# Layer 0's first MLP product by seven products, in two passes, and modulation chunks moved to its second product

## The chip, the cores and the metric

The kernel runs on one core of a Trainium2 chip. The metric is the device time of one execution in microseconds (us), as the median of several runs. PE is the engine for matrix products (its weight loads are shown as PEld), DVE and ACT are the vector and scalar engines, POOL is GpSimd, and SP is the engine whose queue issues the DMAs.

## What is computed

Two layers of a token-mixing sub-layer and an MLP, for 1024 latent tokens and 256 context tokens of 1024 features, in fp32. What the change touches is the MLP and the modulation vectors:

```python
def modulation(cvec, w_mod, b_mod):
    m = jax.nn.silu(cvec) @ w_mod + b_mod
    return jnp.split(m[:, None, :], N_MOD, axis=-1)
...
def sqrelu_mlp(h, w1, w2):
    a = jax.nn.relu(h @ w1)
    return (a * a) @ w2
...
        h2 = modulate(rmsnorm(xl_new, g_pre_mlp[i]), ml[3], ml[4])
        xl_new = xl_new + ml[5] * rmsnorm(sqrelu_mlp(h2, w_mlp_in[i], w_mlp_out[i]), g_post_mlp[i])
```

In layer 0 the MLP runs over the 10 token tiles of 128 (2 of context, 8 latent), in layer 1 over the 8 latent ones. W1 is 1024 x 4096, W2 is 4096 x 1024. Each modulation vector has 6 x 1024 entries for each layer and stream.

## The kernel before

Every fp32 operand is split into a high part, rounded to the type in which PE multiplies at one column per cycle, and a low part; a product is three matmuls (high x high, high x low, low x high, the helper mm3). A `split` is a cast on ACT and a subtraction on DVE.

All operands live in two arenas in SBUF: RT (split operands) and FT (fp32 values). The tables r_outp, r_up, r_down and the F_ tables give the columns of each stage's zones; a zone that is full, or columns that another zone still uses, make an instruction wait.

**Order of the work.** The kernel does not issue instructions as it is written. A Recorder collects them, finds what depends on what (by columns of 32), gives every instruction a cost, and lists them with a list scheduler for each engine (`walk`, eight times forwards and backwards, the best is kept). So the order on each engine is fixed when the kernel is built, and a change in one stage may move instructions in others. DMAs are all on SP's queue, which issues them in its listed order.

**The first MLP product.** In layer 1 it is computed by seven products (Strassen's scheme in Winograd's form, numbered 1 to 7) on pairs of token tiles and pairs of hidden blocks: with four pairs side by side the moving operand is 512 columns wide. W1's operands are made on the way (w1_ops: four sums on DVE and seven splits for each pair of hidden blocks j), `refill` keeps five ready. In layer 0 it is the plain product: for each of 32 hidden blocks f, token chunks of 4, 2 and 4 tiles, 8 x 3 matmuls each. Its token operands are built by `build_hT`, tiles 0 to 4 during the output product and 5 to 9 during the first blocks. In both layers the activations and four sums of them (strassen_sums) are stored to DRAM (actd), and four sums of W2's blocks as well (w2_sums: load, four DVE operations, store to tsd).

**The second MLP product** is seven products in both layers, in four groups g of four j. For each operand set `refill_down` loads activations and weights, splits them and keeps four sets ready; in layer 0 each set serves 5 x 3 matmuls of 512 columns.

**Modulation.** A chunk of 512 modulation columns (mod_task) is 8 loads of w_mod and 8 DVE operations for each stream (csil times a row, accumulated), then a split, matmuls with `pick`, and small transposes. In layer 0's first product twelve tasks run in the background: chunks 10 and 11 of layer 0 and all twelve of layer 1, 0 to 3 for two streams, and 4 to 11 for one. Chunks 0 and 1 are the next layer's first shift, 2 and 3 its scale; 10 and 11 are the gate of the MLP.

Of the kernel before, what the change touches and what calls it, by code (L numbers as in the profile page):

```python
# [46 lines left out]

PATTERN = "qvsvssvvvvsvssvvvvk", "vsvssvvvvsvssvvvvk"
# [8 lines left out]
def r_attn(x, y):  # L57
    return {"V": y, "K": (x[0], x[0] + 7680), "Q": (x[0] + 7680, x[1]), "PT": (28160, 31232), "AW": (31232, 34304), "WE": (20480, 26624), "WX": x, "S": (31232, 34304)}


def r_outp(x, y):
    return {"Y": y, "W": (26624, 28672), "S": (28672, 34304)}


def r_up(x, y):
    return {"Y": y, "X": x, "W": (20480, 34304)}


R_UP_LAST = {"W": (28672, 34304), **{f"H{q}": (7168 * q, 7168 * q + 7168) for q in range(4)}}


def r_down(x, y):
    return {"Y": y, "XT": x, "W": (20480, 34304)}
# [5 lines left out]
F_OUTP = {"Z": (3072, 14848), "C": (14848, 15616), "H": (15616, 16320)}  # L79
F_UP = {"A": (3072, 12032), "W2": (12032, 14080), "M": (14080, 16320), "H": (12032, 16320)}  # L80
F_UP_LAST = {"A": (3072, 10240), "S": (3072, 16320), "T": (10240, 14272), "W2": (14272, 16320)}
F_DOWN = {"Y": (3072, 13312), "H": (13312, 16320), "CS": (3072, 4352)}
# [197 lines left out]
class Arena:  # L280
# [15 lines left out]
    def alloc(self, cols, zone, room=0, top=False):  # L296
        need = -(-max(cols, room) // self.G)
        lo, hi = (c // self.G for c in self.zones[zone])
        if top:
            s = next((s for s in range(hi - need, lo - 1, -1) if not any(self.used[s : s + need])), None)  # L300
            if s is not None:
                return self.take(s, need, cols)
        cur = min(self.cursor.get(zone, lo), hi)
        for a, b in ((cur, hi), (lo, hi)):
# [30 lines left out]
def hybrid_backbone(ctx: ExitStack, tc: tile.TileContext, x, cx, cvec, vecs, lnrow, wmod, win, wq, wkv, wo, w1, w2, cs_tab, cst, out):  # L335
# [150 lines left out]
    def mod_task(l, hc, streams, pool_only=False):  # L486
# [26 lines left out]
        hls = [[R.alloc(512, "PT" if pool_only else "W") for _ in range(2)] for _ in accs]  # L513
# [237 lines left out]
    for l in range(depth):  # L751
# [544 lines left out]
        R.phase(r_outp(*xy))  # L1296
# [11 lines left out]
        HT = NP * P  # L1308

# [31 lines left out]
        tl = blks[0] + blks[1]  # L1341
        lds, mids = [], [wo_first(tl[1], wo_loads(tl[1]))]
        held, stiles, hreg = {}, {}, []

        RH = RT[:, 0:20480].rearrange("p (t s k c) -> p t s k c", t=10, s=2, k=KD)
        RS = RT[:, 0:28672].rearrange("p (q m s k c) -> p q m s k c", q=4, m=7, s=2, k=4)

        def tile_dest(k, grp):
            i = (grp[0] + TB) % 10
            return [RH[:, i : i + len(grp), s, k, :] for s in range(2)]  # L1350

        def pair_tile(q):

            xs = []
            for t in pairs[q]:
                xt = held.pop(t)
                ss, r = st(), st()
                nc.scalar.activation(junk, xt, AF.Square, accum_out=ss)
                rsq(r, ss, D)
                nc.vector.tensor_scalar(xt, xt, r, None, ALU.mult)  # L1360
                xs.append(xt)
            yield
            S = F.alloc(2048, "Z", top=True)
            S4 = S.rearrange("p (b k c) -> p b k c", b=4, k=4)
            A, B = ab_mlp[0]
            for kk in range(4):
                b = bank("hT")
                for i in range(4):
                    k = kk + 4 * (i // 2)
                    nc.tensor.transpose(b[:, i * P : (i + 1) * P], xs[i % 2][:, k * P : (k + 1) * P], ident)  # L1370
                for i in range(2):
                    k = kk + 4 * i
                    nc.scalar.activation(S4[:, 2 * i : 2 * i + 2, kk, :], v3(b[:, i * 256 : (i + 1) * 256], P), AF.Identity, bias=B[:, k : k + 1], scale=A[:, k : k + 1])
                yield
            for xt in xs:
                F.free(xt)
            stiles[q] = S

        def pair_ops(q, zone):

            S = stiles.pop(q)
            b11, b12, b21, b22 = (S[:, i * 512 : (i + 1) * 512] for i in range(4))
            t1, t2, t4 = (F.alloc(512, zone) for _ in range(3))

            def put(m, src):
                hi, lo = (RS[:, q, m - 1, s].rearrange("p k c -> p (k c)") for s in range(2))
                split(hi, lo, src)

            put(1, b11)
            nc.vector.tensor_sub(t1, b12, b11)  # L1390
            put(5, t1)
            nc.vector.tensor_sub(t2, b22, t1)
            put(6, t2)
            put(3, b22)
            nc.vector.tensor_sub(b12, b22, b12)
            put(7, b12)
            put(2, b21)
            nc.vector.tensor_sub(t4, b21, t2)
            put(4, t4)
            for a in (S, t1, t2, t4):  # L1400
                F.free(a)

        if last:
            hreg.append(R.alloc(7168, "Y"))
        else:
            hreg.append(R.alloc(KD * BLK, "Y"))
            s2 = Stream([(w1[l, f], 1, nc.vector) for f in range(2 * NPR)])
            s2.fill(1)
        for i, t in enumerate(tl):
# [14 lines left out]
            keep = last or t < TB  # L1424
            post(y, xt, G[0 if t >= 2 else 1], xmid[l][t * P : (t + 1) * P, :], keep=keep)
            if keep:
                held[t] = y
            if t == 1:
                F.free(G.pop(1))
            if last and t % 2:  # L1430
                builds.add(pair_tile(t // 2 - 1))
                if t == 5:
                    builds.drain()
                    pair_ops(0, "Z")
            elif not last and t < TB and (t % 2 or t == TB - 1):
                grp = [u for u in (t - 1, t) if u in held]
                builds.add(build_hT(None, grp, ab_mlp, tile_dest, "H", lo=nc.vector.tensor_sub, held=held))
# [10 lines left out]
        R.phase(R_UP_LAST if last else r_up(*xy))  # L1448

        def strassen_sums(A):  # L1450

            a11, a12, a22, s1, s2_, s3, s4 = (A[:, i * HT : (i + 1) * HT] for i in range(7))
# [5 lines left out]
        def store_act(j, A):  # L1458
            strassen_sums(A)
            nc.sync.dma_start(out=actd[l][j], in_=A)  # L1460
# [353 lines left out]
```

## Time and profile before

| | us |
|---|---|
| median of 3 runs | 2860.91 |
| their range | 2859.55 to 2861.93 |
| the profiled execution | 2859.87 |
| its span, first to last instruction | 2858.1 |

Stages in the profiled execution: layer 0's output product and first MLP product overlap around 734 us, the second product begins at 1218 us, and layer 1 at about 1573 us; layer 1's first product runs from 2228 to 2520 us and its second one to 2846 us. All instructions are recorded on one source line (L268, the call in `issue`), so the views are read by operation, tile and stretch of time and not by line.

### The profile page before, as it was taken

To read this page: it belongs to the slowest core of one execution; us is meant where nothing else is said; L and a number is where in the kernel's file an instruction comes from. 1 tells how busy PE (TensorE), PEld (TensorE's weight loads), DVE (VectorE), ACT (ScalarE), POOL (GpSimd) and SP (SyncE) were. 2 spreads that over 40 slices of the span, in tenths; PEclk is the share of its full clock that TensorE was granted. 3 is DMA by queue.
4 is the path that set the end of the run, shared out by engine and by line. 5 is a ranking of instruction groups with operands and counts; after the bars stand their busy time and mean duration, and the time that the engine had idled before them with its cause. 6 is when DMAs were issued, how large, how long until landed. Compare 5 with 4: busy or idle time off the path is not lost.

```text
span 2858.1 us, 41182 instructions
## 1 busy us (share of the span) xinstructions
PE 2766.9 (97%) x14978; PEld 2370.8 (83%) x14978; DVE 2143.6 (75%) x3578; ACT 1509.5 (53%) x2907; POOL 349.9 (12%) x363
## 2 busy tenths in 40 slices
PE   7999999989999999999999999999999899999998
PEld 4999888878888888888888799898877788878886
DVE  8988888888766654346666898888888877756777
ACT  6334777776533233353334834677767655554443
POOL 1015364822100000000000201000012000000001
PEclk9999999999999999999999899999999899999999
DMA  7213111254486787575555612000043576686664
GB/s 253 71 33 97 40 50 45 59 169 138 144 285 255 267 314 291 175 260 175 177 175 164 216 56 76 24 16 9 27 160 111 180 269 257 258 335 194 196 192 158
DMA packets 175411, 455.30 MB, mean 159 GB/s; under 512 B 18200, under 2 KB 43368, under 8 KB 167016
## 3 DMA queue, kind: packets, MB, share of 16 engines
q1 hardware_dynamic: 175208, 452.68, 47.2%
q8 instruction: 117, 1.92, 0.3%
q14 instruction: 86, 0.70, 0.1%
HBM read 324.58 MB, written 128.03 MB: 158 GB/s over the span
## 4 chain that ended last, share of the span: by engine, by line
PE 87%; DVE 6%; ACT 3%; DMA 2%; issue 1%; POOL 1%; SPq 0%; DVEq 0%; ACTq 0%
PE PS L268 87%; DVE RT L268 3%; DVE FT L268 2%; ACT FT L268 2%; ACT RT L268 1%; DVE stat L268 1%; POOL stat L268 1%; ACT junk L268 1%; DMA RT<-actd 0%; DMA FT<-in_wo_dram 0%; DMA FT<-in_w_dram 0%; DMA FT<-in_wmod_dram 0%; DMA FT<-atd 0%; SPq L268 0%; DMA FT<-rdd 0%
## 5 line engine op out<-in xcount | busy, mean ns | idle before, releaser
L268 PE MATMUL PS<-RT 128*128 128x512 f32 (+4 forms) x12884 | 2627.6, 359 | 39.1 <-ACT RT L268 19.0
L268 PEld LDWEIGHTS PS<-RT 128*128 128x128 f32 (+1 forms) x12884 | 2154.6, 189 | 373.8 <-ACT RT L268 27.2
L268 DVE TENSOR_TENSOR RT<-FT,RT 128x512 fp32r<-128x512 f32 (+5 forms) x724 | 496.4, 701 | 244.7 <-ACT RT L268 122.5
L268 ACT CAST RT<-FT 128x512 fp32r<-128x512 f32 (+3 forms) x648 | 411.1, 648 | 389.1 <-PE PS L268 312.9
L268 POOL TENSOR_TENSOR stat<-stat,nhalf 128x1 f32<-128x1 f32 (+2 forms) x147 | 125.5, 860 | 1942.0 <-ACT stat L268 1941.5
L268 PE MATMUL PS<-consts,FT 128*128 128x128 f32 (+2 forms) x2008 | 319.1, 275 | 39.1 <-ACT FT L268 15.5
L268 PEld LDWEIGHTS PS<-consts,FT 128*128 128x128 f32 (+2 forms) x2008 | 237.8, 142 | 94.2 <-ACT FT L268 26.9
L268 DVE TENSOR_TENSOR FT<-FT 128x512 f32<-128x512 f32 (+4 forms) x394 | 272.3, 720 | 52.1 <-DMA FT<-in_w_dram 33.6
L268 DVE TENSOR_TENSOR RT<-PS,RT 128x512 fp32r<-128x512 f32 (+3 forms) x409 | 264.5, 660 | 61.8 <-ACT RT L268 52.4
L268 ACT CAST RT<-PS 128x512 fp32r<-128x512 f32 (+3 forms) x409 | 226.1, 567 | 147.7 <-PE PS L268 137.5
L268 DVE TENSOR_TENSOR RT<-RT 128x640 fp32r<-128x640 f32 (+1 forms) x224 | 169.1, 756 | 130.9 <-ACT RT L268 124.6
L268 ACT ACTIVATE FT<-PS,stat 128x1280 f32<-128x1280 f32 (+3 forms) x218 | 216.4, 1003 | 63.3 <-POOL stat L268 25.3
L268 DVE TENSOR_TENSOR FT<-FT,PS 128x512 f32<-128x512 f32 (+3 forms) x350 | 205.5, 618 | 57.0 <-PE PS L268 42.0
L268 ACT CAST RT<-RT 128x640 fp32r<-128x640 f32 (+2 forms) x228 | 155.2, 682 | 161.5 <-DMA RT<-actd 150.6
L268 DVE SCALAR_TENSOR_TENSOR FT<-FT,vec 128x384 f32<-128x384 f32 (+2 forms) x440 | 221.8, 564 | 0.2
L268 ACT COPY FT<-PS 64x256 f32<-64x256 f32 (+9 forms) x258 | 120.0, 473 | 190.9 <-PE PS L268 186.8
L268 DVE TENSOR_REDUCE stat<-PS 128x1 f32<-128x1024 f32 (+1 forms) x200 | 203.9, 1024 | 13.2 <-PE PS L268 12.5
L268 ACT ACTIVATE FT<-PS 128x512 f32<-128x512 f32 (+3 forms) x126 | 65.3, 524 | 199.0 <-PE PS L268 191.7
L268 ACT ACTIVATE FT<-FT 128x512 f32<-128x512 f32 (+2 forms) x162 | 118.7, 736 | 52.0 <-DVE FT L268 49.4
L268 POOL TENSOR_TENSOR FT<-FT,csil 128x512 f32<-128x512 f32 x96 | 104.1, 1085 | 152.1 <-DVE RT L268 79.0
L268 DVE SCALAR_TENSOR_TENSOR FT<-FT,csil 128x512 f32<-128x512 f32 x140 | 99.7, 747 | 28.1 <-DMA FT<-in_wmod_dram 27.4
L268 POOL TENSOR_TENSOR FT<-FT 128x512 f32<-128x512 f32 x84 | 114.2, 1380 | 0.2
(59 smaller groups left out, 718.3 us busy)
## 6 DMA issues: line engine op xcount, KB each, us to landing
FT<-in_wmod_dram SPq DMA_DIRECT2D x160, 256.0 KB, 3.5
actd<-FT SPq DMA_DIRECT2D x16, 2240.0 KB
RT<-actd SPq DMA_DIRECT2D x112, 320.0 KB, 4.7
FT<-in_w_dram SPq DMA_DIRECT2D x64, 512.0 KB, 7.5
FT<-in_w_dram SPq DMA_DIRECT2D x32, 1024.0 KB, 5.6
tsd<-FT SPq DMA_DIRECT2D x32, 1024.0 KB, 8.4
FT<-tsd SPq DMA_DIRECT2D x128, 256.0 KB, 3.5
actd<-FT SPq DMA_DIRECT2D x16, 1792.0 KB, 7.6
```

The source lines that it names most:

```text
L268: r = getattr(getattr(self.nc, eng), name)(*args, **kw)
```

## The change

Layer 0's first product is done by the seven products too. Its pairs are a tile of the second half with one of the first half, (5,0), (6,1), (7,2), (8,3), (9,4). Pairs 0 to 2 are a first pass of 384 columns and pairs 3 and 4 a second pass of 256 columns; W1's operands are made in each pass. The output product takes its tiles in the order 0, 1, 5, 6, 2, 7, 3, 4, 8, 9, and `tile_blocks` builds blocks and operand sets of a pair when both its tiles are there: sets 1, 5, 6 and 3 early, and 7, 2 and 4 when the output product's weights are gone. The second pass's sets are built during the first pass, from xmid, starting at j = 9. W2's sums are spread by the table W2_AT, twelve in the first pass and four in the second, through one buffer of 2048 columns. Layer 1's first product uses the same new builder, with four pairs in one pass.

Of the modulation tasks one (layer 0, chunk 10) stays in the first product. The second product of layer 0 has layer 0's chunk 11 and layer 1's 0 to 9, and both gates and the next layer's affine rows as tasks between them; layer 1's chunks 10 and 11 go to layer 1's second product.

```diff
+W2_AT = {(0, 0): (0, 1), (0, 1): (2,), (0, 2): (3,), (0, 3): (4, 5), (0, 4): (6,), (0, 5): (7,), (0, 6): (8, 9), (0, 7): (10,), (0, 8): (11,), (1, 3): (12,), (1, 6): (13,), (1, 9): (14,), (1, 12): (15,)}
...
+R_OUTP = {"Y": (10240, 19456), "Y2": (31232, 34304), "W": (19456, 20480), "S": (26624, 31232)}
+R_UP = {"SL": (0, 9216), "W": [(9216, 10240), (19456, 23040)], "NY": (23040, 31232), "NX": (10240, 19456)}
...
+        groups = [[0, 1, 2, 3]] if last else [[0, 1, 2], [3, 4]]
...
+        MS = (1, 5, 6, 3, 7, 2, 4)
+        early = {1: "Y", 5: "Y"} if last else {1: "Y", 5: "Y", 6: "Y", 3: "Y2"}
...
+        def put(q, m):
+
+            g, i = place[q]
+            bl = blocks[q]
+            b11, b12, b21, b22 = bl
+            if m in (5, 6, 4):
+                nc.vector.tensor_sub(b11, {5: b12, 6: b22, 4: b21}[m], b11)
+            hi, lo = (slots[g][m][:, i * D + n * 512 : i * D + (n + 1) * 512] for n in range(2))
+            split(hi, lo, {3: b22, 7: b12, 2: b21}.get(m, b11))
+            if m == 3:
+                nc.vector.tensor_sub(b12, b22, b12)
...
-            for hc in range(10, 12):
-                mods.add(mod_task(0, hc, (0, 1)))
-            for hc in range(0, 4):
-                mods.add(mod_task(l + 1, hc, (0, 1)))
-            for hc in range(4, 12):
-                mods.add(mod_task(l + 1, hc, (0,)))
...
-            chunks_ = [(slice(5, 9), 1, 4), (slice(4, 10, 5), None, 2), (slice(0, 4), 0, 4)]
...
+            for l_, hc in ((l, 10),):
+                mods.add(mod_task(l_, hc, (0, 1), "NY"))
+        n_, start_next, n_next = 0, 9, 4
+        for g, grp in enumerate(groups):
+            w = len(grp) * P
...
+                for mi, (m, c) in enumerate(((1, 0), (5, 1), (6, 0), (3, 1), (7, 0), (2, 2), (4, 0))):
+                    refill(5 if last else 4)
...
+                        for n, (a, v) in enumerate(((wh, bh), (wh, bl), (wl, bh))):
+                            nc.tensor.matmul(v3(bs[c], P), a[:, s], v, start=m in (1, 5, 2) and kk + n == 0, stop=kk + n == 5, skip_group_check=True)
...
+                store_act(j, grp, A)
+                for j_ in (j,) if last else W2_AT.get((g, j), ()):
+                    w2_sums(j_)
...
+        if last:
+            for hc in (10, 11):
+                mods.add(mod_task(l, hc, (0,), "W"))
+        else:
+            ab_next = []
+            mods.add(mod_task(l, 11, (0, 1), "W"))
+            mods.add(both_gates())
+            for hc in range(4):
+                mods.add(mod_task(l + 1, hc, (0, 1), "W"))
+            mods.add(next_affine())
+            for hc in range(4, 10):
+                mods.add(mod_task(l + 1, hc, (0,), "W"))
```

PE's list where layer 0's first product begins, before (RT are split operands, PS is PSUM, 128x256 the output; the last transposes of the token tiles stand first):

```order
L268 MATMUL PS<-consts,FT 128x128 x2
L268 MATMUL PS<-RT 128x512 x9
L268 MATMUL PS<-RT 128x256 x24
L268 MATMUL PS<-RT 128x512 x24
L268 MATMUL PS<-RT 128x256 x24
L268 MATMUL PS<-RT 128x512 x24
```

And of the change, from the last tile of the output product to the first modulation task (its matmuls read `pick`):

```order
L267 MATMUL PS<-consts,FT 128x128 x6
L267 MATMUL PS<-RT 128x512 x48
L267 MATMUL PS<-RT 128x384 x223
L267 MATMUL PS<-RT,pick 2x512
L267 MATMUL PS<-RT 128x384 x51
```

The plain product began among transposes of its own token tiles; the new one begins after the last of them, and no other matmul of the output product stands behind it. Where the passes meet, and the second product begins, the change has on PE:

```order
L267 MATMUL PS<-RT 128x384 x114
L267 MATMUL PS<-RT 128x256 x7
L267 MATMUL PS<-RT 128x384 x10
L267 MATMUL PS<-RT 128x256 x7
L267 MATMUL PS<-RT 128x384 x2
L267 MATMUL PS<-RT 128x256 x1330
L267 MATMUL PS<-RT 128x512 x181
```

The first matmuls of the second pass stand among the last of the first, and the second product follows the second pass directly. SP's list in layer 0's first product, before (in_w is W1 with 128x1024 and W2 with 128x2x1024):

```order
L268 DMA actd_79<-FT 128x4480
L268 DMA FT<-in_wmod_dram 128x512
L268 DMA tsd_81<-FT 128x2048
L268 DMA FT<-in_wmod_dram 128x512 x2
L268 DMA FT<-in_w_dram 128x1024
L268 DMA FT<-in_w_dram 128x2x1024
L268 DMA FT<-in_wmod_dram 128x512 x2
L268 DMA FT<-in_w_dram 128x1024
L268 DMA FT<-in_wmod_dram 128x512 x3
L268 DMA actd_79<-FT 128x4480
```

And of the change, in the first pass:

```order
L267 DMA FT<-in_w_dram 128x1024 x2
L267 DMA actd_79<-FT 896x1x384
L267 DMA tsd_81<-FT 128x2048
L267 DMA FT<-in_w_dram 128x2x1024
L267 DMA FT<-in_w_dram 128x1024 x2
L267 DMA actd_79<-FT 896x1x384
L267 DMA tsd_81<-FT 128x2048
L267 DMA FT<-in_w_dram 128x1024
L267 DMA FT<-in_w_dram 128x2x1024
```

The modulation loads are gone from between them, one round of W2 sums stands to nearly each store of activations, and activations are stored in runs of 384 columns.

## Rows read from the trace of the kernel before

**Rows 1.** The page's first part: busy us, share of the span and instructions of each engine (PEld is the weight loads of PE).

```profile
PE 2766.9 (97%) x14978; PEld 2370.8 (83%) x14978; DVE 2143.6 (75%) x3578; ACT 1509.5 (53%) x2907; POOL 349.9 (12%) x363
```

**Rows 2.** Busy time by stretch: the output product of layer 0, its end with the first MLP product, and the second one. Columns: stretch, its us; busy us and instructions of PE, PEld, DVE, ACT, POOL; granted clock as a share, DMA share, GB/s.

```profile
630.00:734.00 104.00, 104.00 (x526) 85.32 (x525) 90.52 (x189) 69.69 (x202) 28.20 (x42) 1.00 0.46 145
734.00:1218.00 484.00, 483.88 (x2532) 407.32 (x2530) 276.85 (x416) 169.84 (x273) 10.67 (x26) 1.00 0.71 254
1236.00:1560.00 324.00, 324.00 (x1431) 268.36 (x1431) 200.41 (x298) 128.98 (x208) 0.00 (x0) 1.00 0.60 179
```

**Rows 3.** The chain of waits in order of time: start, us, what. It is the piece that covers the first MLP product and the beginning of the second.

```profile
850.18 383.77 PE PS L268 x1990
```

**Rows 4.** PE's timeline: start us, us, engine, line, operation, tiles, form of the first, count. Two stretches of the first product between modulation tasks (138 matmuls, 90 of 512 and 48 of 256 columns), runs of 256 and 384 columns in the projections, and a long run there whose forms average 320 columns; each with the row that follows it.

```profile
854.06 26.50 PE L268 MATMUL PS<-RT 128*128 128x512 f32 x138
880.51 0.40 PE L268 MATMUL PS<-RT,pick 128*2 128x512 f32 x1
...
884.19 26.49 PE L268 MATMUL PS<-RT 128*128 128x512 f32 x138
910.52 0.40 PE L268 MATMUL PS<-RT,pick 128*2 128x512 f32 x1
...
85.54 36.76 PE L268 MATMUL PS<-RT 128*128 128x320 f32 x249
122.14 0.59 PE L268 MATMUL PS<-FT,consts 128*128 128x256 f32 x2
...
179.25 3.11 PE L268 MATMUL PS<-RT 128*128 128x256 f32 x24
182.19 0.82 PE L268 MATMUL PS<-consts,FT 128*128 128x128 f32 x6
182.77 4.43 PE L268 MATMUL PS<-RT 128*128 128x384 f32 x24
187.03 0.38 PE L268 MATMUL PS<-consts,FT 128*128 128x128 f32 x2
```

**Rows 5.** DVE's timeline, same columns: runs of instructions back to back, each with the row that follows it.

```profile
798.28 2.73 DVE L268 SCALAR_TENSOR_TENSOR FT<-FT,csil 128x512 f32<-128x512 f32 x4
...
800.93 2.89 DVE L268 TENSOR_TENSOR FT<-FT 128x640 f32<-128x640 f32 x4
...
1217.93 1.55 DVE L268 TENSOR_TENSOR RT<-RT 128x640 fp32r<-128x640 f32 x2
1219.40 2.29 DVE L268 TENSOR_TENSOR FT<-FT 128x640 f32<-128x640 f32 x3
...
2240.17 3.70 DVE L268 TENSOR_TENSOR RT<-FT,RT 128x512 fp32r<-128x512 f32 x6
2243.79 0.68 DVE L268 TENSOR_TENSOR FT<-FT,PS 128x512 f32<-128x512 f32 x1
```

**Rows 6.** Groups of instructions by form over the whole span: count, then busy us and mean ns of one, then idle before.

```profile
L268 PEld LDWEIGHTS PS<-RT 128*128 128x128 f32 x12820 | 2150.0, 189 | 345.8 <-ACT FT L268 15.5 <-ACT RT L268 15.2 <-DVE RT L268 7.3
...
L268 DVE TENSOR_TENSOR RT<-FT,RT 128x512 fp32r<-128x512 f32 x446 | 306.1, 697 | 180.9 <-ACT RT L268 81.8 <-PE PS L268 72.4 <-issue 20.3
...
L268 DVE TENSOR_TENSOR RT<-FT,RT 128x256 fp32r<-128x256 f32 x114 | 48.4, 449 | 4.5 <-ACT RT L268 4.3
```

**Rows 7.** SP's timeline in layer 1's first product, one block of pairs (in_w is W1 and W2, tsd the store of W2's sums).

```profile
2426.84 0.33 SPq L268 DMA_DIRECT2D tsd<-FT  x1
2427.44 7.63 SPq L268 DMA_DIRECT2D FT<-in_w_dram  x2
2443.22 0.33 SPq L268 DMA_DIRECT2D actd<-FT  x1
...
2445.88 0.33 SPq L268 DMA_DIRECT2D tsd<-FT  x1
```

**Rows 8.** From the views of the tiles tsd and in_w in layer 1's first product (2220 to 2530 us): us from issue to landing of a store of W2's sums, and of a load of W1 or W2.

```profile
DMA to landing us min/median/max: 7.7/8.4/9.1
...
DMA to landing us min/median/max: 4.9/6.1/8.5
```

**Rows 9.** Busy time by stretch, columns as in rows 2: the start of layer 1's first product.

```profile
2208.00:2229.00 21.00, 7.16 (x30) 4.72 (x29) 18.27 (x28) 15.53 (x33) 2.69 (x2) 0.71 0.38 141
```

**Rows 10.** The same, for layer 0's projections and attention, and for layer 1's with its output product.

```profile
60.00:620.00 560.00, 535.86 (x3561) 487.55 (x3560) 490.03 (x859) 332.57 (x669) 235.08 (x206) 0.99 0.22 66
...
1620.00:2208.00 588.00, 575.53 (x3668) 523.68 (x3667) 502.24 (x887) 374.01 (x771) 44.10 (x55) 1.00 0.20 65
```

**Rows 11.** SP's timeline in layer 0's first product: the first stores of W2's sums.

```profile
784.36 0.33 SPq L268 DMA_DIRECT2D tsd<-FT  x1
...
803.85 0.33 SPq L268 DMA_DIRECT2D tsd<-FT  x1
...
824.13 0.33 SPq L268 DMA_DIRECT2D tsd<-FT  x1
...
845.18 0.33 SPq L268 DMA_DIRECT2D tsd<-FT  x1
```

More of the change, by code (lines that the diff above doesn't have):

```diff
@@ L294, in phase, with alloc @@
         self.cursor = {}
-    def alloc(self, cols, zone, room=0, top=False):
+    def alloc(self, cols, zone, room=0):
         need = -(-max(cols, room) // self.G)
[L298 to L304, printed above, removed]
+        z = self.zones[zone]
+        z = [(lo // self.G, hi // self.G) for lo, hi in (z if isinstance(z, list) else [z])]
+        cur = self.cursor.get(zone, 0)
+        for a, b in [(max(lo, cur), hi) for lo, hi in z] + z:
             run = 0
@@ L511, in mod_task @@
             yield
-        hls = [[R.alloc(512, "PT" if pool_only else "W") for _ in range(2)] for _ in accs]
+        hls = [[R.alloc(512, rzone) for _ in range(2)] for _ in accs]
         for a, hl in zip(accs, hls):
@@ L1295, in hybrid_backbone @@
         F.free(CS)
[L1296 removed]
+        R.phase(R_OUTP_LAST if last else R_OUTP)
         F.phase(F_OUTP)
@@ L1339, in post @@
                 F.free(y)
-        tl = blks[0] + blks[1]
+        tl = blks[0] + blks[1] if last else [0, 1, 5, 6, 2, 7, 3, 4, 8, 9]
         lds, mids = [], [wo_first(tl[1], wo_loads(tl[1]))]
[L1343 to L1350, printed above, removed]
@@ new lines, in tile_blocks @@
+        def tile_blocks(t, y, zone, then):
+            q, i = next((q, p.index(t)) for q, p in enumerate(pairs) if t in p)
+            A, B = ab_mlp[0 if t >= 2 else 1]
+            if y is None:
+                y = F.alloc(D, zone)
+                nc.sync.dma_start(out=y, in_=xmid[l][t * P : (t + 1) * P, :])
+            ss, r = st(), st()
+            nc.scalar.activation(junk, y, AF.Square, accum_out=ss)
+            rsq(r, ss, D)
+            nc.vector.tensor_scalar(y, y, r, None, ALU.mult)
+            if q not in blocks:
+                blocks[q] = []
+                for _ in range(4):
+                    blocks[q].append(F.alloc(512, zone))
@@ L1362, in pair_tile @@
             yield
[L1363 to L1366, printed above, removed]
+            for h in range(2):
                 b = bank("hT")
[L1368 to L1373, printed above, removed]
-                yield
@@ L1409, in hybrid_backbone, with refill @@
+        ready, gen = deque(), (o for g in range(len(groups)) for o in w1_ops(g))
+        def refill(n):
+            while len(ready) < n:
+                o = next(gen, None)
+                if o is None:
+                    break
+                ready.append(o)
+        for m, zone in early.items():
+            slot(0, m, zone)
+        refill(1)
         for i, t in enumerate(tl):
@@ L1423, in hybrid_backbone @@
                     R.free(a)
-            keep = last or t < TB
+            keep = any(t in pairs[q] for q in groups[0])
             post(y, xt, G[0 if t >= 2 else 1], xmid[l][t * P : (t + 1) * P, :], keep=keep)
-            if keep:
-                held[t] = y
             if t == 1:
                 F.free(G.pop(1))
[L1430 to L1437, printed above, removed]
+            if keep:
+                builds.add(tile_blocks(t, y, "Z", early))
         builds.drain()
@@ L1678, in finish @@
                 held[t] = y
-        if not last:
-            ab_next = [affine_of(l + 1, 0, s) for s in range(2)]
+        n_ = 0
         for g in range(NPR // GP):
```

262 lines of the change are left out of this document (112 added, 150 removed).

## The prediction

> **What bounds the kernel now.** I read the page first: PE is busy for 97% of the span, DVE for 75% [rows 1]. A share over the span settles nothing about one stage, so I cut the trace into stages next. From 734 to 1218 us, the end of layer 0's output product and the whole first MLP product, PE is busy for 483.88 of 484.00 us at the full granted clock (2.4 GHz), while DVE works 276.85 and the DMA engines are at 0.71 [rows 2]. From 1236 to 1560, the second product, PE is busy 324.00 of 324.00 us and DVE 200.41 [rows 2]. The chain of waits agrees: 383.77 us of it, from 850 on, are PE alone [rows 3]. So in the stage that changes PE has no idle time to win; only less PE work can shorten it, and any wait that the change brings is paid in full.
>
> **The matmuls removed.** Each of 32 hidden blocks is multiplied with 4 + 2 + 4 token tiles: 24 x 2 matmuls of 512 columns and 24 of 256. That is 1536 and 768 in all. Durations of single matmuls overlap (they are modelled latencies), so I take start to start: two stretches of 138 matmuls, 90 wide and 48 narrow, last 880.51 - 854.06 = 26.45 and 910.52 - 884.19 = 26.33 us, mean 26.39. A run of 24 of 256 lasts 182.19 - 179.25 = 2.94 us, 0.1225 each; that leaves (26.39 - 48 x 0.1225) / 90 = 0.2279 for 512 [rows 4]. Removed: 1536 x 0.2279 + 768 x 0.1225 = 350.1 + 94.1 = 444.1 us.
>
> **The matmuls added.** Seven products of 12 matmuls for each of 16 blocks of pairs, once 384 wide and once 256 wide: 1344 of each. At 256: 1344 x 0.1225 = 164.6. At 384 there are three readings. On the line from 256 to 512 (0.412 ns per column) it is 0.1752, so 235.5 us. The one clean run of 24 lasts 187.03 - 182.77 = 4.26 us, 0.1775 each, so 238.6, but it carries the switch to transposes at its end. The long run of 249 whose widths average 320 gives 36.60 / 249 = 0.147 [rows 4], which puts 384 at 0.1733, so 232.9. I take 0.1752: 400.1 us, and **PE work falls by 44.0 us**, between 40.9 and 46.6. By columns alone it would be an eighth of 444.1, 55.5; the 384 additional instructions give the rest back. The modulation matmuls are equally many and only move.
>
> The Trainium skill (TensorE: Matmul & The Clock Gate, Back-to-back issue gap) gives N / 2.4 + 2.5 ns for an isolated warm matmul: 109, 163 and 216 ns at the three widths, an estimate of 50 us saved. The trace disagrees, 122.5 ns and 227.9 ns in runs where each matmul has its own weight load, and the measurement decides.
>
> **DVE in the second pass.** A block of the second pass takes PE 84 x 0.1225 = 10.29 us. DVE does for it 7 low parts and 4 operand sums of 512 columns, and 3 additions from PSUM and 4 sums of 256. Back to back, 512 columns cost (3.70 - 0.69 for its last) / 5 = 0.602 us, and 640 cost 1219.40 - 1217.93 = 1.47 for two, 0.735 [rows 5]; the slope puts 256 at 0.336 and 384 at 0.469. So 11 x 0.602 + 7 x 0.336 = 8.97 us, and the four weight sums of this pass add 16 x 0.602 / 16 = 0.60: 9.57 of 10.29, 93%. By full durations, 0.697 and 0.449 [rows 6], it is 11 x 0.697 + 7 x 0.449 + 0.70 = 11.5 us, 1.2 too much in each of 16 blocks, 19 us in all. The order lets independent instructions follow each other, so the back-to-back row is nearer: I take +3 us for chains within a block, and keep 0 and 19 as ends. The first pass is looser: 16 x (11 x 0.602 + 7 x 0.469) = 158.5, twelve weight sums 28.9, one modulation chunk about 12 and four early operand sets of the second group about 10, 209 of 235.5 us.
>
> **Loads and stores in the first pass.** SP issues in order, and the W2 buffer holds one tile of 2048 columns: a load of W2 waits until the store of the previous sums has landed, and behind it stand the W1 loads that feed PE and the store of the activations. One round in layer 1, which has the same buffer, is: store at 2426.84, next load at about 2427.44 + 7.63 - 0.33 = 2434.74, so 7.90 us [rows 7]; landing of a load 6.1 us in the median [rows 8]; four sums 2.4. Together 16.4 us. The new SP order places twelve of these stores, eleven rounds, within twelve blocks of 84 x 0.1752 = 14.72 us: 16.06 us per round. It lags by 11 x 0.34 = 3.7 us, and four prepared operand pairs of 12 matmuls each, 4 x 2.10 = 8.4 us, cover that: 0. Landings at the worst of [rows 8], 9.1 and 8.5, make a round 20 us; that end stays for the rivals.
>
> [...]
>
> **The starts of the stages.** Four token tiles of the output product, which the second group needs, come last, 4 x 48 x 0.2279 = 43.8 us, and hide the first four operand sets of group one. Sets 7, 2 and 4 need the room of the output weights; the first of them has 4 products, 8.4 us, before PE asks for it. I take +1 us; the other end is layer 1's own start, where PE works 7.16 of 21.00 us [rows 9], 13.8 idle. Between the passes the new order mixes the first products of pass two among the last of pass one: 0. Layer 1's start changes its builder (tile by tile instead of by pairs, operand set by operand set for all pairs); the chain through the last tile's norm stays, so 0, between -4 and +4.
>
> **The modulation chunks in the second product.** There are 128 DVE instructions with csil at (800.93 - 798.28) / 4 = 0.66 us [rows 5] and 16 low parts: 94 us on top of 62% of about 340 us, 90%. From 630 to 734 DVE was busy 90.52 of 104.00 us and PE did not idle at all [rows 2], so 0; with less cover it is a few us. Their loads wait on SP for a PE bank, and loads of operands stand behind them, four operand sets ahead of use (4 x 15 x 0.2279 = 13.7 us of PE). Layer 1's second product receives two chunks, 16 such instructions and 2 low parts, about 12 us of DVE, and its gate is written three products before its end: 0.
>
> The planner orders the whole program anew, attention and projections too. PE idles there for 24.1 and 12.5 us [rows 10]; I allow 4 us either way.
>
> **Sum.** The profiled execution took 2859.87 us (span 2858.1), 1.0 below the median and inside the range of the runs, so nothing is corrected. 2859.87 - 44.0 + 3 + 1 = **2820 us**.
>
> **The rivals.**
> *DVE sets the pace of the second pass.* For it: 93% is more than the 87% of any stretch in [rows 2]. Against: these instructions have few dependences and ACT is free. Price 19 in place of 3: 2836 us.
> *The single W2 buffer sets the pace of the first pass, and the kernel is slower.* Rounds longer than 16.06 us delay the W1 loads behind them on SP, and PE stops once 8.4 us are used up. The gain of 40 is gone when 11 rounds lag 48.4 us, from 20.5 us per round on. For it: in layer 0 today the stores follow each other after 19.5, 20.3 and 21.05 us [rows 11], with modulation loads on SP between them. Against: those loads go, save one chunk, and layer 1 shows 19.04 us where PE, not the buffer, sets the pace. At 21.05 us: 11 x 4.99 - 8.4 = 46.5, so 2866 us.
> *The narrow matmuls don't pay, since each needs a weight load*, whose rows last 0.189 us in the mean [rows 6]: 2688 x 0.189 = 508, 64 more than before, 2924 us. The run of 24 at 0.1225 speaks plainly against it, since loads are as many as matmuls [rows 1].
> *More is won*: 46.6 of PE work, layer 1's start 4 and the new order 2 better: 2807 us.
>
> **Chances.** Forecast, 2810 to 2829: 0.63. DVE pace, 2829 to 2845: 0.22. W2 buffer: 0.06; weight loads: 0.01. More won: 0.08. The range 2807 to 2842 runs from the last case to the low saving (40.9) with the DVE end, 2859.87 - 40.9 + 19 + 4, and leaves out about 0.14. A difference below 0.2% (5.7 us) can't be told from none. Of the two slow cases 0.03 lie within that, 0.04 are slower; all else is faster: 0.93.
>
> **What would show it.** PE between the start of the first product and the second should be busy without gaps for about 400 us, in stretches of 84 matmuls of 14.7 and 10.3 us. DVE should show over 90% in the second pass, and PE waits on DVE there mean the first rival. W2 stores over 17 us apart, with PE waiting for ACT or DVE that wait for W1 loads, mean the second. The second product should stay at its 340 us with DVE near 90%. I am wrong if PE idles over 20 us in layer 0's MLP, or if 384 columns cost more than 0.18 us.

## The result, and the profile after

The changed kernel takes 2838.6 us (median of 4 runs, 2833.7 to 2840.2), the kernel before 2860.6; the ratio is 0.992, 95% interval 0.9903 to 0.9937. That is 22 us faster where 40 were forecast; it lies within the range of 2807 to 2842. The profiled execution took 2837.1 us (span 2835.4).

The page's first part, to be read beside [rows 1]: 384 more matmuls, 33 us less of PE, and 222 us more of DVE.

```profile
PE 2734.2 (96%) x15362; PEld 2384.8 (84%) x15362; DVE 2365.9 (83%) x4017; ACT 1684.1 (59%) x3422; POOL 352.5 (12%) x363
```

Milestones that both traces have (stores on SP, and the last matmul of 512 columns in layer 0's second product) tell where the time went, in us:

| Stretch | before | after | difference |
|---|---|---|---|
| start to the last attention store (atd) of layer 0 | 636.9 | 632.2 | -4.7 |
| to the last xmid store of layer 0 | 120.9 | 131.4 | +10.5 |
| to the last matmul of layer 0's second product | 839.1 | 813.6 | -25.5 |
| to the last atd store of layer 1 | 517.4 | 518.2 | +0.8 |
| to the last xmid store of layer 1 | 100.7 | 104.6 | +3.9 |
| to the first output store | 617.5 | 609.3 | -8.2 |
| to the last output store | 22.0 | 22.5 | +0.5 |

The stages around layer 0's MLP nearly cancel out (+2.8 in all). The miss is in the third row: 25.5 us won in place of 40.

PE's timeline in layer 0's first product, columns as in [rows 4]; brackets hold the idle time before a row and what ended it.

```profile
758.44 0.61 PE L267 MATMUL PS<-RT 128*128 128x384 f32 x2 [0.36 <-ACT RT L267]
759.71 2.03 PE L267 MATMUL PS<-RT 128*128 128x384 f32 x10 [0.66 <-DVE RT L267]
762.70 0.62 PE L267 MATMUL PS<-RT 128*128 128x384 f32 x2 [0.95 <-ACT RT L267]
764.78 17.18 PE L267 MATMUL PS<-RT 128*128 128x384 f32 x96 [1.47 <-DVE RT L267]
...
814.30 123.01 PE L267 MATMUL PS<-RT 128*128 128x384 f32 x706
938.01 25.25 PE L267 MATMUL PS<-RT 128*128 128x384 f32 x144 [0.70 <-DVE FT L267]
...
983.70 2.29 PE L267 MATMUL PS<-RT 128*128 128x384 f32 x6 [3.36 <-ACT FT L267]
...
1052.64 50.66 PE L267 MATMUL PS<-RT 128*128 128x256 f32 x420 [0.17 <-DVE FT L267]
...
1103.59 56.42 PE L267 MATMUL PS<-RT 128*128 128x256 f32 x468 [0.29 <-DVE FT L267]
```

Two long runs give the prices of the new matmuls: 123.01 / 706 = 0.174 us at 384 columns (0.1752 forecast) and 50.66 / 420 = 0.121 at 256 (0.1225). PE's work fell by 444.1 - 1344 x (0.174 + 0.121) = 48 us. So 22 of 48 were given back, and the windows show where, with the columns of [rows 2]:

```profile
735.00:800.00 65.00, 60.41 (x311) 54.08 (x309) 60.18 (x99) 37.38 (x82) 4.49 (x6) 1.00 0.61 205
800.00:950.00 150.00, 149.25 (x858) 147.65 (x858) 132.40 (x230) 91.14 (x188) 0.83 (x1) 1.00 0.83 301
950.00:1010.00 60.00, 54.40 (x306) 52.65 (x305) 48.20 (x83) 49.02 (x112) 2.06 (x3) 0.94 0.55 188
1010.00:1060.00 50.00, 48.65 (x395) 47.92 (x394) 46.71 (x91) 38.70 (x91) 0.00 (x0) 1.00 0.73 247
1060.00:1160.00 100.00, 99.70 (x829) 99.31 (x828) 97.47 (x191) 75.58 (x177) 0.00 (x0) 1.00 0.75 251
1160.00:1235.00 75.00, 73.32 (x386) 62.00 (x386) 56.65 (x94) 47.18 (x93) 1.33 (x4) 1.00 0.91 315
1235.00:1540.00 305.00, 302.18 (x1342) 243.80 (x1341) 258.42 (x396) 125.75 (x208) 2.63 (x11) 1.00 0.72 233
```

PE was gapless here before [rows 2]. Now it idles 4.6 us at the start of the first pass (735 to 800), 5.6 where the passes meet (950 to 1010), 1.4 and 1.7 at two later places and 2.8 in the second product. In the second pass PE is busy for 99.70 us of the 100 from 1060 on, although DVE is busy for 97% of them. Where the passes meet the clock costs more:

```profile
970.00:982.40 12.40, 10.07 (x61) 9.45 (x59) 9.69 (x16) 12.40 (x31) 0.96 (x1) 1.00 0.13 44
982.40:989.20 6.80, 5.50 (x20) 5.40 (x21) 3.63 (x6) 6.80 (x19) 0.55 (x1) 0.50 0.34 119
```

PE had been busy for 10.07 of 12.40 us, ACT for all of them; then 6.8 us were granted at 0.50 (1.2 GHz). PE was busy for 5.50 of these, and half of that, some 2.7 us, is what the lower clock cost. With it the losses add up to some 19 of the 22 us.

**The start.** DVE's timeline, the columns of [rows 5]. The first product begins at 755.5 us. From 758 to 765 PE twice waits for a rounded part (ACT RT) and two matmuls later for a low part (DVE RT). A product goes high x high, high x low, low x high with W1's part named first, so a missing operand of W1 stops PE at the first and the third matmul, a missing token set at the first and the second. These are then most likely W1's operands, of which the kernel prepares one ahead (`refill(1)`); the trace doesn't name them. The token sets 7, 2 and 4, which come last in a block of 84 matmuls, were there in time: 28 matmuls stand before 764.78, and the next 96 run without a wait.

```profile
761.31 1.82 DVE L267 TENSOR_TENSOR FT<-FT 128x512 f32<-128x512 f32 x2
763.04 0.48 DVE L267 TENSOR_SCALAR FT<-FT,csil 128x512 f32<-128x512 f32 x1
763.44 0.68 DVE L267 TENSOR_TENSOR FT<-FT 128x512 f32<-128x512 f32 x1
764.04 0.68 DVE L267 TENSOR_TENSOR RT<-FT,RT 128x512 fp32r<-128x512 f32 x1
764.65 0.48 DVE L267 TENSOR_SCALAR FT<-FT,csil 128x512 f32<-128x512 f32 x1
765.04 0.68 DVE L267 TENSOR_TENSOR FT<-FT 128x512 f32<-128x512 f32 x1
```

Between the low parts (RT<-FT,RT) that PE needs stand the modulation chunk (csil), sums (FT<-FT; those of W1 and W2 have the same form) and the last addition of the output product (the second of the first row, 1024 columns).

**Where the passes meet.** SP's timeline: the first and the last two stores of W2's sums in the first pass, then the loads of the second group's tiles (xmid).

```profile
771.89 0.33 SPq L267 DMA_DIRECT2D tsd<-FT  x1
...
937.52 0.33 SPq L267 DMA_DIRECT2D tsd<-FT  x1
...
952.21 0.33 SPq L267 DMA_DIRECT2D tsd<-FT  x1
957.77 0.33 SPq L267 DMA_DIRECT2D FT<-xmid  x1
...
967.28 10.79 SPq L267 DMA_DIRECT2D FT<-xmid  x2
```

The eleven rounds take (952.21 - 771.89) / 11 = 16.4 us each, as forecast. But the second group's tiles are built in a zone (NT) that contains the W2 buffer, so three of their four loads come after its last store, at 958 to 978 us of a pass that ends at 1013. The first of these waits 5.2 us for that store to land, the longest such wait in SP's view of waits from 940 to 1000 us (us in total, times, longest):

```profile
SPq L267 <- DMA tsd<-FT: 9.6, 2, 5.2
```

The last, at 977.75, follows a transpose of the tile before (977.44). ACT then has them in a heap:

```profile
979.50 2.31 ACT L267 ACTIVATE FT<-PS,B,A 128x128 f32<-128x128 f32 x6
981.56 1.19 ACT L267 ACTIVATE junk<-FT 128x1024 bf16<-128x1024 f32 x1
982.50 0.34 ACT L267 ACTIVATION_READ_ACCUMULATOR junk<-FT 128x1 f32 x1
982.60 0.59 ACT L267 ACTIVATE FT<-PS,B,A 128x128 f32<-128x128 f32 x1
982.94 0.34 ACT L267 ACTIVATE stat<-stat 128x1 f32<-128x1 f32 x1
983.03 0.62 ACT L267 COPY FT<-PS 128x384 f32<-128x384 f32 x1
```

The copy at 983.03 empties a PSUM bank; PE, idle for 3.36 us, goes on at 983.70. The tiles' scaling (PS,B,A) and a norm stood before it.

### The profile page after: what moved, and what is told of

Read it like the earlier page. It is cut to its first block, busy times and chain, and to the rows that moved or that the text cites. A ratio compares the mean times of both kernels' runs of the same rounds, so it can differ in the third digit from the quotient of the medians.

```text
span 2835.4 us, 43024 instructions
## 1 busy us (share of the span) xinstructions
PE 2734.2 (96%) x15362; PEld 2384.8 (84%) x15362; DVE 2365.9 (83%) x4017; ACT 1684.1 (59%) x3422; POOL 352.5 (12%) x363
## 4 chain that ended last, share of the span: by engine, by line
PE 79%; DVE 8%; DMA 6%; ACT 5%; issue 2%; POOL 1%; SPq 0%; DVEq 0%; ACTq 0%
PE PS L267 79%; DVE RT L267 3%; DVE FT L267 3%; ACT FT L267 3%; DMA FT<-in_w_dram 2%; ACT RT L267 2%; DMA tsd<-FT 1%; DVE stat L267 1%; DMA RT<-actd 1%; POOL stat L267 1%; DMA actd<-FT 1%; ACT junk L267 1%; DMA FT<-rdd 0%; DMA FT<-in_wmod_dram 0%; DMA xmid<-FT 0%
## 5 line engine op out<-in xcount | busy, mean ns | idle before, releaser
L267 PE MATMUL PS<-RT 128*128 128x512 f32 (+4 forms) x13268 | 2588.9, 350 | 59.8 <-DVE RT L267 22.7
L267 ACT CAST RT<-FT 128x512 fp32r<-128x512 f32 (+4 forms) x875 | 535.6, 628 | 421.1 <-PE PS L267 311.6
L267 DVE TENSOR_TENSOR RT<-FT,RT 128x512 fp32r<-128x512 f32 (+6 forms) x903 | 612.8, 693 | 136.8 <-PE PS L267 56.4
L267 DVE TENSOR_TENSOR FT<-FT 128x512 f32<-128x512 f32 (+4 forms) x606 | 378.9, 650 | 52.6 <-DMA FT<-in_w_dram 26.7
L267 PE MATMUL PS<-consts,FT 128*128 128x128 f32 (+1 forms) x2008 | 311.7, 275 | 25.9 <-ACT FT L267 13.0
L267 PEld LDWEIGHTS PS<-consts,FT 128*128 128x128 f32 (+1 forms) x2008 | 236.0, 142 | 77.7 <-ACT FT L267 23.2
L267 DVE TENSOR_TENSOR FT<-FT,PS 128x512 f32<-128x512 f32 (+4 forms) x446 | 252.4, 587 | 35.7 <-PE PS L267 22.2
L267 ACT COPY FT<-PS 64x256 f32<-64x256 f32 (+7 forms) x354 | 161.3, 460 | 175.5 <-PE PS L267 168.6
L267 ACT ACTIVATE FT<-FT 128x256 f32<-128x256 f32 (+2 forms) x354 | 177.8, 519 | 101.9 <-DVE FT L267 97.6
L267 ACT ACTIVATE junk<-FT 128x1024 bf16<-128x1024 f32 (+1 forms) x92 | 86.2, 937 | 44.3 <-DVE FT L267 27.9
```

Source lines behind the costliest of these rows:

```text
L267: r = getattr(getattr(self.nc, eng), name)(*args, **kw)
```

## The experiments

"Pass one" is the time from the first to the last matmul of 384 columns, "pass two" from there to the last of 256, "MLP" the third row of the table above; all from the traces, in us. The time is the median of the runs, the other columns are of one profiled execution, whose own time is up to 4.2 us away from it (e2 below, e7 above). In the changed kernel, e4 and e9, 14 matmuls of pass two (1.7 us) stand before the end of pass one. The forecast of the two passes was 400.

| Kernel | time | pass one | pass two | MLP |
|---|---|---|---|---|
| before | 2860.6 | | | 839.1 |
| after | 2838.6 | 257.6 | 163.9 | 813.6 |
| e1, no W2 work | 2819.6 | 238.1 | 166.2 | 797.2 |
| e2, seven sums, earlier building | 2834.5 | 246.3 | 166.8 | 806.9 |
| e3, layer 1's builder alone | 2862.2 | | | 839.1 |
| e4, twelve orders tried | 2836.1 | 258.0 | 161.6 | 812.4 |
| e5, W2 rounds without sums | 2821.0 | 241.3 | 165.1 | 798.4 |
| e6, W2 sums without stores | 2826.5 | 248.7 | 166.5 | 803.1 |
| e7, W2 in halves | 2841.6 | 263.1 | 170.5 | 824.4 |
| e8, chunk moved, two W2 buffers | 2822.1 | 240.6 | 168.8 | 801.7 |
| e9, chunk moved, one buffer | 2827.2 | 248.1 | 163.3 | 808.1 |
| e10, all sums in pass one | 2829.7 | 247.9 | 163.5 | 806.7 |
| e11, e8 with sums on POOL | 2820.9 | 241.2 | 166.7 | 803.5 |
| e12, e8 with seven sums | 2825.1 | 241.7 | 167.7 | 803.7 |

**e1: no W2 work in layer 0.**

```diff
-W2_AT = {(0, 0): (0, 1), (0, 1): (2,), ...}
+W2_AT = {}
...
+                if m in t_at and not last:
+                    src = w2[l, 2 * j * P : (2 * j + 1) * P, 512 * (m % 2) : 512 * (m % 2) + 512]
```

> The changed kernel without the W2 sums of layer 0 (left out: the 64 sums and their stores; the second product reads a quarter of W2 in place of each, so the traffic of that stage is the same). Theory A, the twelve W2 rounds of the first pass hold the buffer in which the second group's tiles are built, so these are built in one heap at 957 to 990 us, where PE loses some 10 us by idling and at half clock: the loss between 955 and 1010 falls below 3 us, DVE falls below 90% in the second pass, and the time is 2826 to 2831 us. Rival B, the heap is made by the planner, which puts this work as late as its ranks allow, whatever the buffer does: the loss between the passes stays at 8 to 10 us and the time is 2834 to 2840 us.

2819.6 us (ratio 0.9853, 0.9839 to 0.9866), less than either theory had. Windows of e1, start and meeting of the passes:

```profile
735.00:800.00 65.00, 65.00 (x352) 61.22 (x351) 60.43 (x100) 40.39 (x88) 6.37 (x7) 1.00 0.45 148
...
950.00:1010.00 60.00, 60.00 (x390) 60.00 (x389) 49.53 (x88) 43.06 (x90) 0.00 (x0) 1.00 0.55 184
```

Both losses are gone: A was right about the place where the passes meet, and the start hangs on the W2 work too, which neither theory had. DVE fell less than A said: 91.53 of 100 us in the second pass.

**e2: seven sums in pass one, building from block 6.**

```diff
-..., (0, 3): (4, 5), (0, 4): (6,), (0, 5): (7,), (0, 6): (8, 9), (0, 7): (10,), (0, 8): (11,), (1, 3): (12,), ...
+..., (0, 3): (4,), (0, 4): (5,), (0, 5): (6,), (1, 0): (7,), (1, 2): (8,), (1, 4): (9,), ...
-        n_, start_next, n_next = 0, 9, 4
+        n_, start_next, n_next = 0, 6, 4
```

> Seven W2 sums in the first pass in place of twelve, nine in place of four in the second; the building of the second group may begin at block 6 in place of 9. Theory A: the tiles of the second group come some 50 us sooner and are spread out, the loss between the passes falls from 10 us to 3 or less; five more sums on DVE (12 us on 164 us, where it is over 90% busy) take back 3 to 8 us of it: 2832 to 2838 us. Rival B: the loss between the passes stays, and the second pass gets longer as well: 2841 to 2847 us.

2834.5 us, as A said. The last three tile loads are issued at 883, 892 and 901 us, and the window where the passes meet has no idle time:

```profile
950.00:1010.00 60.00, 60.00 (x374) 60.00 (x373) 50.74 (x89) 41.49 (x85) 0.00 (x0) 1.00 0.63 215
```

The start still loses 3.4 us there, and pass two is 1 us longer when the 1.7 us above are counted with it. The time alone doesn't separate e2 from the changed kernel: the intervals of the ratio overlap (0.9891 to 0.9918, and 0.9903 to 0.9937).

**e3: the kernel before with layer 1's new builder.** Layer 0 and the chunks keep the old text:

```diff
+        if not last:
+            R.phase(B_r_outp(*xy))
...
+        else:
             R.phase(R_OUTP_LAST if last else R_OUTP)
```

> The kernel before with one part of the change: layer 1's output product and first product are written as in the changed kernel, layer 0 and all modulation chunks as before. Theory C, the 9 us that layer 1's output product and MLP gained in the changed kernel come from its new builder: 2850 to 2854 us, with the gain after 2115 us. Rival D, they come from another order that the planner happened to find, or from the chunks that moved: 2858 to 2863 us.

2862.2 us, ratio 1.0001 (0.9992 to 1.001): D. The builder costs 3.8 us in layer 1's output product and wins 3.3 in its MLP. The other 4.9 of the 8.2 us there come from something else in the change; which part is open.

**e4: the same operations, twelve orders tried.**

```diff
-        for _ in range(8):
+        for _ in range(12):
```

> The changed kernel with the same operations, where the planner tries twelve orders in place of eight and keeps its best. Theory E, the order in stages that the change doesn't touch (projections, attention) is worth several us either way, which is where 6 us of the forecast went: the time moves by 3 to 10 us from 2838.6, and the sections up to 650 us and from 1600 to 2100 us move with it by 3 us or more. Rival F, the orders are as good as each other and those 6 us are a cost of the change: within 2 us of 2838.6, and each section within 2 us.

2836.1 us; its interval (0.9899 to 0.9926) covers most of that of the changed kernel. All stretches but one lie within 1.2 us of those of the changed kernel; layer 1's MLP is 3.3 shorter. That is nearer to F. Of the other kernels e10 and e11 have another order on PE from 281 us on and reach the last atd store of layer 0 at 632.9 and 628.8 us. Eight kernels (e1, e2, e5 to e9, e12) have the order of the changed kernel on every engine up to 615 us, and with it they reach that store at 630.1 to 634.0. So another order is worth little more than single traces differ by, and E isn't shown.

**e5 and e6: the rounds without the sums, and the sums without the stores.** e5:

```diff
-            nc.vector.tensor_sub(b11, b12, b11)
+            if last:
+                nc.vector.tensor_sub(b11, b12, b11)
...
```

> The changed kernel where layer 0's W2 tiles are loaded and stored as before, through the same single buffer, but the 64 subtractions between are left out. It splits the 19 us that leaving out the whole W2 work gave. Theory A, the rounds of the buffer cost the time: 16 rounds of some 14 us in place of 16.4 remain, so most of the 19 us stays lost: 2832 to 2838 us. Rival G, DVE's share costs it (64 x 0.60 = 38 us of DVE in a stage where it is over 90% busy): the gain is had here too, 2819 to 2824 us.

e6, with the same reading of W2 as e1:

```diff
-            nc.sync.dma_start(out=tsd[l][j], in_=t)
+            if last:
+                nc.sync.dma_start(out=tsd[l][j], in_=t)
```

> The opposite: layer 0's W2 tiles are loaded and summed, but not stored (left out; the second product reads a quarter of W2 in place of each sum). The buffer comes free after 6.1 + 2.4 = 8.5 us in place of 16.4, and 1 MB a round less is moved; DVE does the same as in the changed kernel. Theory A: the rounds end by about 870 us, the second group is built early, 2820 to 2826 us. Rival G: DVE still has all its work, 2833 to 2839 us.

2821.0 and 2826.5 us: G in e5, and in e6 just above A's range. Each half alone costs little beside e1, 1.4 and 6.9 us; together they cost 19. With either half gone the tile loads come earlier (929 to 952 and 905 to 929 us, after 958 to 978) and the meeting of the passes is whole: PE is busy for 60.00 and 59.53 of 60 us. At the start PE idles 1.5 us without the sums, but still 5.5 with them and no stores: there DVE's sums are at fault.

**e7: W2 in halves through the same room.**

```diff
-            t = F.alloc(2048, "W2")
+            for c in (0, 256):
+                t = F.alloc(D, "W2")
...
```

> The whole computation. Each W2 tile goes through the same room in two halves of 1024 columns, so that one half is loaded while the other is stored; 128 subtractions of 256 columns (0.336 us) in place of 64 of 512 (0.602), 4.5 us of DVE more, and three DMAs a half. Theory A: the rounds overlap, the last of the first pass ends some 60 us sooner, the loss between the passes goes: 2826 to 2834 us. Rival G: nothing is gained, DVE has more work: 2839 to 2845 us.

2841.6 us, as G said. Windows:

```profile
735.00:800.00 65.00, 56.49 (x283) 50.24 (x282) 58.93 (x107) 32.69 (x70) 4.30 (x6) 0.97 0.60 200
800.00:950.00 150.00, 143.57 (x797) 138.27 (x796) 128.68 (x252) 87.45 (x184) 1.40 (x2) 0.98 0.87 291
950.00:1010.00 60.00, 60.00 (x355) 59.90 (x354) 53.19 (x93) 52.55 (x119) 1.58 (x2) 1.00 0.59 192
```

The passes meet without a gap, though the last store is only 17 us earlier (935 us). The start and the blocks after it lose 15 us. There are more DVE instructions and more transfers on SP; which of them costs it wasn't separated.

**e8 and e9: the modulation chunk moved to the second product; e8 also a second W2 buffer in its room.** e8 (e9 leaves the line of F_UP as it was):

```diff
-            for l_, hc in ((l, 10),):
-                mods.add(mod_task(l_, hc, (0, 1), "NY"))
...
-"W2": (3072, 5120)
+"W2": (3072, 7168)
...
-            mods.add(mod_task(l, 11, (0, 1), "W"))
+            for hc in (10, 11):
+                mods.add(mod_task(l, hc, (0, 1), "W"))
...
-                        mods.tick(1 + (n_ % 3 == 0))
+                        mods.tick(1 + (n_ % 5 in (0, 2)))
```

> The whole computation. The first pass's modulation chunk goes to the second product with the others, and its room makes a second W2 buffer. Theory A: two rounds overlap, and with the chunk (12 us of DVE in the first pass) gone the loss at the start and between the passes falls by 8 us or more; the second product gets a 16th more DVE work and loses 0 to 2 us: 2828 to 2834 us. Rival G: only the 12 us of DVE help: 2836 to 2839 us.

> The 2822 us version with its second W2 buffer taken away again: against the changed kernel only the first pass's modulation chunk is moved to the second product. It splits those 16.5 us. Theory G, DVE's work in the first product is what costs (the chunk is 12 us of it): most of the gain stays, 2822 to 2828 us. Theory A, the single buffer holds up the second group's tiles: the heap at 957 to 990 us is back and most of the gain goes, 2832 to 2838 us.

2822.1 us (0.9862, 0.9848 to 0.9876), better than A had it, and 2827.2 (0.9883, 0.9868 to 0.9898), within G's range. By the times the chunk is worth 11.4 us and the second buffer 5.1; by the MLP column it is 5.5 and 6.4. The rest of the chunk's share lies outside the MLP, where single traces differ, and the two intervals overlap a little, so how the 16.5 us divide is known only roughly. Pass one got 9.5 us shorter without the chunk, the second product 4 us longer with it. The chunk's share also holds the faster ticking in the second product, which wasn't tried by itself. The meeting of the passes in e8, and in e9, where loads come at 948 to 970 us again, followed by e9's second pass:

```profile
950.00:1010.00 60.00, 60.00 (x384) 60.00 (x383) 50.98 (x91) 42.80 (x89) 0.00 (x0) 1.00 0.61 201
```

```profile
950.00:1010.00 60.00, 56.07 (x349) 53.64 (x348) 51.29 (x91) 51.67 (x122) 2.05 (x3) 1.00 0.54 185
...
1060.00:1160.00 100.00, 100.00 (x836) 100.00 (x835) 98.49 (x191) 76.21 (x179) 0.00 (x0) 1.00 0.79 265
```

The last row is the plainest on DVE's pace: 98.49 of 100 us busy, and PE gapless beside it.

**e10: all sixteen sums in pass one.** On e8:

```diff
+W2_AT = {(0, 0): (0,), (0, 1): (1, 2), (0, 2): (3,), (0, 3): (4, 5), (0, 4): (6, 7), (0, 5): (8,), (0, 6): (9, 10), (0, 7): (11, 12), (0, 8): (13, 14), (0, 9): (15,)}
...
+        n_, start_next, n_next = 0, 10, 4
```

> The 2822 us version (two W2 buffers) with all sixteen W2 sums in the first pass, in its first ten blocks, and the second group's building from block 10. Theory G, DVE sets the pace of the second pass (97% busy there): with 10 us of its work gone from the second pass the losses there fall from 9 us to 3 or less, and the first pass (DVE at 91%) takes them with 0 to 2 us: 2814 to 2819 us. Rival H, the losses in the second pass are single late instructions that have nothing to do with the load: 2820 to 2824 us, or more if the first pass overflows.

2829.7 us, 7.6 more than e8. Pass two got 5.3 us shorter, as G has it, and pass one 7.3 longer, the overflow that H allows for. That the 5.3 are DVE's isn't shown: e1, with no sums at all, has 166.2 in pass two. PE idles 2.8 us from 800 to 950, with the DMA engines at 0.95:

```profile
800.00:950.00 150.00, 147.16 (x832) 144.68 (x832) 132.53 (x230) 91.08 (x187) 0.75 (x1) 0.99 0.95 339
```

**e11: the activations' sums of pass two on POOL.** On e8:

```diff
+            e = nc.gpsimd if g and not last else nc.vector
-            nc.vector.tensor_add(s1, s3, a22)
+            e.tensor_add(s1, s3, a22)
...
```

> The 2822 us version with the four sums per block of the activations on POOL in the second pass, which takes 64 x 0.336 = 21 us off DVE there. Theory G: the losses of the second pass fall from 9 us to 3 or less: 2814 to 2819 us. Rival H: 2820 to 2824 us. Rival I, POOL's work slows DVE down: DVE's 512-column subtractions in the second pass take longer than 0.69 us in the mean, and the time is 2823 us or more.

2820.9 us, no different from e8: H in the time, and I in the instructions (last section). But DVE wasn't relieved, and so the run doesn't test G; windows of e8 and of e11:

```profile
1060.00:1160.00 100.00, 96.67 (x789) 96.06 (x789) 92.98 (x180) 71.58 (x168) 0.00 (x0) 0.98 0.71 235
```

```profile
1060.00:1160.00 100.00, 96.38 (x785) 94.44 (x783) 93.64 (x140) 70.78 (x169) 43.17 (x40) 1.00 0.70 232
```

DVE has 140 instructions in place of 180 and is busy for as long.

**e12: e8 with seven sums in pass one, nine in pass two.**

```diff
+W2_AT = {(0, 0): (0, 1), (0, 1): (2,), ..., (0, 5): (6,), (1, 0): (7,), (1, 2): (8,), ...}
...
+        n_, start_next, n_next = 0, 6, 4
```

> The 2822 us version (two W2 buffers in the first pass, its modulation chunk in the second product) with seven W2 sums in the first pass and nine in the second, whose own W2 buffer stays single, and the second group's building from block 6. Theory J, what costs is DVE work and W2 rounds in the first pass, while the second pass can take more of both (one version had DVE busy for 98.5% there and PE for 100%): the first pass gets down from 241 us towards 237, the second stays at 164 to 169 us: 2815 to 2820 us. Rival K, the second pass has no room left, nine rounds through one buffer delay it by 4 us or more, and nothing is won: 2821 to 2828 us.

2825.1 us, in K's range but not for K's reason: pass two is no longer than e8's. The 3.0 us to e8 are within the intervals of the ratio (0.9859 to 0.9894 for e12). Pass one didn't get shorter than e8's; what is left there is the start, 2.5 us idle and a clock of 0.97:

```profile
735.00:800.00 65.00, 62.54 (x324) 57.68 (x323) 58.51 (x97) 37.86 (x82) 6.02 (x6) 0.97 0.58 203
```

## Why the prediction was half right

The time lies in the range, but between 2829 and 2845, where the prediction had its rival on DVE's pace (chance 0.22, 2836 us), and that rival's mechanism wasn't the cause. The 19 us that the range allowed for DVE were used up by other losses; as far as the mechanism goes, that the range held is luck. By the windows PE idled 17 us in layer 0's MLP, just under the 20 that the prediction named as a sign of being wrong.

**Matmuls removed and added: right.** 48 us less PE work where 44.0 were forecast.

**DVE in the second pass: right.** Forecast 93% busy and +3 us; from 1060 to 1160 us it was 97%. Pass two took 165.6 us with the 14 matmuls that stand before it, against 162.6 of pure work at 0.121: 3 us lost. The rival that DVE sets its pace falls by e9's row. A share of 97% or 98% here adds up durations that overlap, 0.687 us each in e8 where instructions follow each other after 0.60.

**Loads and stores in the first pass: the step that failed.** The round of 16.4 us was met exactly, and the W1 loads behind it didn't starve PE, as the rival had it. But "cover that: 0" asked only who stands behind the load on SP. It didn't ask who waits for the buffer itself: the building of the second group, whose zone contains it. So "Between the passes ... 0" was wrong as well: some 8 us, 5.6 idle and 2.7 by the clock. e2 (earlier building) and e8 (second buffer) take that loss away by different means, and e9 brings part of it back.

**Starts of the stages: under-sized.** +1 was taken, 4.6 us measured. The step counted how long four products cover the token sets 7, 2 and 4, and these came in time. It left out W1's operands, most of which are made only when the first product begins, and what DVE does meanwhile: W2's sums and the chunk stand among them. Without the sums the loss is 0 and 1.5 us (e1, e5), without the chunk 2.8 (e9). The remark "209 of 235.5" on the first pass was a mean; DVE was busy 60 of the first 65 us, and in e1, where PE has no gap there, as well. So its order mattered there, not its load.

**Modulation chunks: nearly right.** From the last matmul of 256 columns to its end the second product took 383.2 us before and 400.0 in the changed kernel. Of the 17 us, 11 are modulation matmuls and small transposes, which only moved (32 at 0.234 us and 44 at 0.084, start to start); 2 are more idle time of PE, where the forecast was 0, and the rest is open. With a chunk more it took 399.8 us in e8 and 403.1 to 404.2 in e9 to e12; the other kernels with the change took 395.9 to 401.9. The chunk that stayed in the first pass cost that pass 9.5 us (e9).

**Layer 1 and the planner.** Layer 1's start "0, between -4 and +4": +3.9 in the output product and -8.2 in the MLP; of these the builder gives +3.8 and -3.3 (e3), near nothing together. For the new order 4 us were allowed either way. Up to the last xmid store of layer 0 the changed kernel lost 5.8 us, 4.7 won in the attention and 10.5 lost behind it; the forecast has no term for this, and what of it is the order and what the new work of the output product is open.

Open stays how 1.4 and 6.9 us make 19. That both are needed to push the last tiles to 978 us fits the load times, but wasn't tried apart from them.

## What to carry to other kernels

For each buffer with a long round trip, list everything that shares its columns, not only what is queued behind its transfers: the next user starts when the last round has landed. Where a forecast rests on a mean share, look at the two ends of the stage, where preparation for the next work is heaped on the engines that also feed PE. A stage can run at 98% on a second engine without a loss, and lose 8 us in the 60 us in which a burst stands ahead of one copy that frees a bank.

## What the runs showed of the hardware

POOL's additions slowed those DVE instructions that read two operands in SBUF. DVE from 1010 to 1160 us in e8, and below it DVE and POOL in e11: out<-in, count, then busy us and mean ns of one, idle before.

```profile
L267 DVE TENSOR_TENSOR RT<-FT,RT 128x512 fp32r<-128x512 f32 x102 | 69.6, 687 | 4.5 <-ACT RT L267 1.8 <-PE PS L267 1.2 <-issue 0.7
L267 DVE TENSOR_TENSOR FT<-FT 128x512 f32<-128x512 f32 x67 | 45.5, 686 | 4.7 <-DMA FT<-in_w_dram 4.7
...
L267 DVE TENSOR_TENSOR FT<-FT,PS 128x256 f32<-128x256 f32 x42 | 17.4, 415 | 0.3 <-PE PS L267 0.2
```

```profile
L267 DVE TENSOR_TENSOR RT<-FT,RT 128x512 fp32r<-128x512 f32 x100 | 77.0, 793 | 6.4 <-ACT RT L267 4.2 <-PE PS L267 1.5 <-ACT FT L267 0.2
L267 DVE TENSOR_TENSOR FT<-FT 128x512 f32<-128x512 f32 x65 | 53.1, 830 | 1.4 <-DMA FT<-in_w_dram 1.4
L267 DVE TENSOR_TENSOR FT<-FT,PS 128x256 f32<-128x256 f32 x44 | 18.0, 411 | 2.4 <-PE PS L267 1.5 <-POOL FT L267 0.7
...
L267 POOL TENSOR_TENSOR FT<-FT 128x256 f32<-128x256 f32 x57 | 61.8, 1104 | 88.1 <-ACT FT L267 86.5 <-POOL FT L267 0.7
```

Subtractions with two operands in SBUF went from 687 to 793 ns, sums of 512 columns from 686 to 830; additions with one operand in PSUM stayed at 415 and 411. So most of what was taken off DVE came back as longer instructions: 100 x 0.106 + 65 x 0.144 = 20 us in these 150. The Trainium skill (Advanced Engine Details and Errata, VectorE Performance Modes) says that VectorE's second SBUF port is shared with GpSimd and that two-port instructions and GpSimd's block each other. The rows agree that the two engines get in each other's way, but for another kind of instruction: the section's table gives tensor_tensor no two-port mode, and here it is plain fp32 tensor_tensor with two SBUF operands that got longer. For two-port instructions these rows show nothing.
